# A hybrid decoder step on one core: GpSimd's share of the mixer goes to VectorE

## The chip, the core and the metric

The kernel runs on one core of one Trainium2 chip. The core has TensorE (PE in the rows; its weight loads are PEld), VectorE (DVE), ScalarE (ACT), GpSimd (POOL) and SyncE (SP), which here only issues transfers. The metric is device time in microseconds (us) of one execution. Line numbers such as L716 are those of the kernel before.

## The reference, cut to what matters

One layer of a decoder, in float32, for 256 prompt tokens and 8 x 8 sampled tokens, 320 in all: a half feed-forward, a mixer, and another half feed-forward.

```
h = x + 1/2 * SwiGLU_1(RMSNorm(x))
z = RMSNorm(h) @ w_in      -> q | k | v | conv pair a, b
A: 16 heads of 64, three dilated patterns (128,1), (512,4), (2048,16);
   sampled queries read cache_k, cache_v (8 x 2048 rows of 1024)
B: u = a * sigmoid(b); causal depthwise conv of 31 taps; LayerNorm; swish
h = h + concat(A, B) @ w_out
y = h + 1/2 * SwiGLU_2(RMSNorm(h))
```

## The kernel before, in words

**Products.** Features lie on the partitions, the 320 tokens beside each other. A weight piece is loaded by SyncE (`raw`, L276), rounded by ScalarE (`wh`, L238), and the rest is formed by VectorE (`wl = raw - wh`, L239); TensorE then does three matmuls per tile (L299 to L301). A piece is 128x1024 in the feed-forwards and 128x512 in the mixer. The mixer's pieces have four `raw` buffers and three pairs `wh`, `wl`, so a late `wl` holds back both TensorE and the next load. Counted over the whole program, pieces 281 to 312 make k, 313 to 376 the conv pair, 377 to 408 v, 409 to 440 the half of w_out that multiplies the conv branch, and 441 to 472 the other half.

**Beside the products.** After every piece of k, conv, v and of w_out's first half, `pump` puts some steps of the sampled tokens' attention and five entries of `bg`, the convolution's list, into the program. One step of attention is one tile of 128 cache rows, 512 KB. A *far* tile (L511 to L513, six per batch, ring `kf` of three buffers) holds keys that one query each sees: GpSimd multiplies it with the query `qr` (L512) and VectorE sums over the head (L513). A *near* tile goes through TensorE (L534 to L547), a value tile too (`vn`, L610, L614). Between batches come the softmax (L562 to L571) and two spread products `af` and `px` on GpSimd (L520, L571).

**The convolution.** For each of eight channel tiles, 21 taps are `cacc += w * u` on VectorE (L716; the first is L714); ten are products on ScalarE (L721), added up by GpSimd (L725, L749). The sampled tokens' taps are one product of 992 columns on GpSimd (L734) and a sum on VectorE (L736), twice per tile. Behind the last tile stand the steps of the LayerNorm: sums over the tiles (L810, even tiles on VectorE, odd ones on GpSimd), mean, centring (L826), root (L834, L836), scaling (L839) and swish (L840). Only then can w_out's first half begin: its operands are the split conv tiles `ch`, `cl` (L238, L239).

**The rest of GpSimd's work in the mixer.** The products with the norm's root and with the sine for q and k (L447, L455), a copy of the sampled columns (L458), the gate's product (L791), half of the scaling (L839), and clearing and filling a small tile `z` (L568, L569).

**Order.** The program is recorded in the order above; a scheduler then sets each engine's fixed order with a timeline of its own, attention steps first (their priority is raised), `bg` behind. Each engine works its list strictly in that order.

Of the kernel before, what the change touches and what calls it, by code (L numbers as in the profile page):

```python
# [22 lines left out]
TD = 8  # L23
# [19 lines left out]
PTAPS = 10  # L43
# [32 lines left out]
def shape_constants():  # L76
    """Tables that depend on the shapes alone, side by side in one array."""
    parts = []

    def put(name, a):  # L80
        off = sum(p.shape[1] for p in parts)
        _CW[name] = (off, a.shape[1])
        parts.append(np.ascontiguousarray(a, dtype=np.float32))

    p = np.arange(P)
    put("ident", np.eye(P))
    put("blk64", (p[:, None] // HD == p[None, :] // HD) / HD)
    inv = np.power(np.float32(10000.0), -np.arange(HD // 2, dtype=np.float32) / np.float32(HD // 2)).astype(np.float32)
    pos = np.concatenate([np.arange(SEQ), np.tile(PAST + np.arange(TD), NB)]).astype(np.float32)
    ang = (inv[p % (HD // 2)][:, None] * pos[None, :]).astype(np.float32).astype(np.float64)  # L90
    sgn = np.where(p % HD < HD // 2, -1.0, 1.0)[:, None]
    put("cos", np.cos(ang))
    put("sin", np.sin(ang) * sgn)
    q = np.arange(P)[:, None]
    put("pmask", np.concatenate([_bias(q - np.arange(P)[None]), _bias(P + q - np.arange(2 * P)[None])], 1))
    t = (p % TD)[:, None]
    idx = np.concatenate([FAR + np.arange(NNEAR * P), PAST + np.arange(TD)])
    far = 16 * np.arange(NFAR * 16)
    put("smask", np.concatenate([_bias(PAST + t - idx[None, :]), _bias(PAST - far[None, :] + 0 * t)], 1))
    put("tmask", t == np.arange(TD)[None, :])  # L100
    put("msel", (p // TD)[:, None] == np.arange(16)[None, :])
    f = np.arange(256)
    put("dmask", (p // TD % 4)[:, None] == (f // HD)[None, :])
    put("sel", ((p // 32 * TD + p % TD)[:, None] == np.arange(32)[None, :]))
    return np.concatenate(parts, 1)
# [5 lines left out]
def block(ctx, tc, A, O):  # L111
# [41 lines left out]
    class Norm:  # L153
        """Deferred RMSNorm: x*g goes on (split) at once, the reciprocal root is applied to the products."""
# [57 lines left out]
    def tables():  # L212
        """The other gains and the taps of the convolution, features on the partitions."""
# [34 lines left out]
    def defer(n, fn):  # L248
        """Trace fn n weight pieces further on, so that the tensor engine has work while its operands are made."""
        later.append([n, fn])  # L250
# [12 lines left out]
    class Feed:  # L263
        """Weight pieces of nkp row tiles x 256 columns in the order of their use: loads run la pieces ahead of the
        products, splits ls pieces."""
# [22 lines left out]
    def gemm(feed, nk, hi, lo, evac, after=None):  # L288
        """Two column tiles of the weights (nk row tiles) times the split activations."""
# [108 lines left out]
    # fixed buffers in turn: their users follow in the order of the program  # L398
# [12 lines left out]
    # the rows of the conv state that stay  # L411
    nc.sync.dma_start(O["new_conv_sample"][0][:, 0:ST - TD, :], A["state_conv"][0][:, TD:ST, :])

# [1 line left out]
    def out3(src, dsts):  # L415
        """Three token blocks of a [feature, token] tile, transposed, to dsts."""
# [11 lines left out]
    if True:  # L428
# [12 lines left out]
        def qk_norm(i, zq, sq, goff, is_q, d):  # L441
# [5 lines left out]
            nc.gpsimd.tensor_tensor(zq, zq, sd, op=ALU.mult)  # L447
# [7 lines left out]
            nc.gpsimd.tensor_tensor(rot, rot, sin, op=ALU.mult)  # L455
            r = rp.tile([P, T], F32, name="qk", bufs=5)
            nc.vector.tensor_tensor(r, t1, rot, op=ALU.add)
            nc.gpsimd.tensor_copy((qsT if is_q else ksT)[:, i, :], r[:, SEQ:T])  # L458
# [23 lines left out]
    sa = mix.enter_context(tc.tile_pool(name="sa", bufs=2, side="right"))  # L482
    ck = A["cache_k"][0].rearrange("b s h d -> b s (h d)")
# [20 lines left out]
    def far_scores(b, out):  # L504
        """Row p of a far tile holds keys that only query p % 8 sees: products on the vector engines."""
# [3 lines left out]
        for n in range(NFAR):  # L509
            kn = sa.tile([P, AW], F32, name="kf", bufs=3)  # L510
            nc.sync.dma_start(kn, rows(ck, b, n))  # L511
            nc.gpsimd.tensor_tensor(kn, kn, qr, op=ALU.mult)  # L512
# [5 lines left out]
    def far_sums(S, sf):  # L518
        af = sa.tile([P, NFAR * 16, TD], F32, name="af", bufs=1)
        nc.gpsimd.tensor_tensor(af, bc(sf), tmb, op=ALU.mult)  # L520
# [38 lines left out]
    def soft(S):  # L559
# [7 lines left out]
        z = sa.tile([P, 2 * TS - TD], F32, name="z")  # L567
        nc.gpsimd.memset(z, 0.0)  # L568
        nc.gpsimd.tensor_copy(z[:, TS - TD:TS], sm[:, SNEW:SFAR])  # L569
        px = sa.tile([P, NFAR * 16, TD], F32, name="px", bufs=1)  # L570
        nc.gpsimd.tensor_tensor(px, bc(sm[:, SFAR:SW]), tmb, op=ALU.mult)  # L571
# [52 lines left out]
    def late_values():  # L624
        """The new keys' part of the batches whose rows came before v was there."""
# [68 lines left out]
    cst = ExitStack()  # L694
    cp = cst.enter_context(tc.tile_pool(name="cp", bufs=2))
    cprod = deque(cp.tile([P, 384], F32, name=f"cprod{i}", bufs=1) for i in range(3))
    csum = deque(cp.tile([P, 384], F32, name=f"csum{i}", bufs=1) for i in range(2))
# [8 lines left out]
    def conv_taps(i, u):  # L706
        a = cacc[i]
        ap, bias = a[:, 0:SEQ], gains[:, DWB + i:DWB + i + 1]
        s2 = {}

        def tap(j):
            w, src = dww[:, i, j:j + 1], u[:, j:j + SEQ]
            if j == 0:
                nc.vector.tensor_scalar(ap, src, w, bias, op0=ALU.mult, op1=ALU.add)  # L714
# [3 lines left out]
        def ptap(j):  # L718
            first = "c" not in s2
            t = turn(csum if first else cprod)[:, 0:SEQ]  # L720
            nc.scalar.activation(t, u[:, j:j + SEQ], AF.Copy, bias=0.0, scale=dww[:, i, j:j + 1])  # L721
            if first:
                s2["c"] = t
            else:
                nc.gpsimd.tensor_tensor(s2["c"], s2["c"], t, op=ALU.add)  # L725

        def stap(h):
            """The decoded tokens of four batches: all taps of their windows at once."""
# [5 lines left out]
            nc.gpsimd.tensor_tensor(pr4, win, w, op=ALU.mult)  # L734
# [5 lines left out]
        nd = CW - PTAPS  # L740
        for j in range(nd):
            bg.append(lambda j=j: tap(j))
            k = (j + 1) * PTAPS // nd - j * PTAPS // nd
            for x in range(k):
                bg.append(lambda x=j * PTAPS // nd + x: ptap(nd + x))
            if j in (3, 9):
                bg.append(lambda j=j: stap(j > 3))
        def close():
            nc.gpsimd.tensor_tensor(ap, ap, s2["c"], op=ALU.add)  # L749
            norm_add("m", a, i)  # L750

        bg.append(close)
# [22 lines left out]
    def conv_in(g, after):  # L775
# [7 lines left out]
        def ev_b(j, ps):  # L783
# [7 lines left out]
            nc.gpsimd.tensor_tensor(uc, at[j], t, op=ALU.mult)  # L791
# [10 lines left out]
    def norm_add(key, x, i):  # L802
        """Sums over the channel tiles, the even ones on one engine, the odd ones on the other."""
        e = nc.gpsimd if i % 2 else nc.vector
        k = key + str(i % 2)
        if i < 2:
            norm[k] = tmp.tile([P, T], F32, name="n" + k, tag=("ssa", "sd")[i % 2], bufs=1)
            e.tensor_copy(norm[k], x)
        else:
            e.tensor_tensor(norm[k], norm[k], x, op=ALU.add)  # L810

    def norm_mean(key):
        m = mtile("mu")
        for i in range(2):
            nc.tensor.matmul(m[:, 0:T], onesC, norm[key + str(i)], start=i == 0, stop=i == 1)
        return m[:, 0:T]

    def conv_norm():
# [19 lines left out]
        def act(i):  # L838
            (nc.gpsimd if i % 2 else nc.vector).tensor_tensor(cacc[i], cacc[i], s["r"], op=ALU.mult)  # L839
# [179 lines left out]
```

## Time and profile before

| | |
|---|---|
| time, median of 3 runs | 2650.08 us (2642.7 to 2655.48) |
| profiled execution, its span | 2650.1 us |
| TensorE busy | 2536.2 us, 96% |
| VectorE busy | 1445.5 us, 55% |
| ScalarE busy | 1031.1 us, 39% |
| GpSimd busy | 447.6 us, 17% |
| granted TensorE clock, mean | 0.980 |

The profiled execution's span equals the median to 0.1 us, so a sum made against the span can be read as a sum against the median. Shares over the whole span say little: the feed-forwards lie before about 970 us and after about 1710 us, with TensorE busy throughout, and the mixer between them looks different. It is read stage by stage.

### The profile page before, as it was taken

The numbers are of one execution on the slowest core, as the hardware profiler recorded it, in microseconds if no ns is written. First come the engines' busy times: TensorE is split into PE (matmuls) and PEld (weight loads), VectorE is DVE, ScalarE is ACT, GpSimd is POOL, SyncE is SP. The second block draws the span as 40 slices with busy tenths as digits, with TensorE's granted clock in tenths as the row PEclk, the third lists the DMA queues.
The fourth block names the chain that finished last, engine by engine and source line by source line (L and its number), as shares of the span: only waits on it lengthen the run. The fifth ranks groups of instructions, "written<-read, shape, count | busy, mean of one in ns | idle before, by whom it ended". The sixth has DMA issues, their size and how long they took to land. (4 is left out here: it accounts for less than half of the span.)

```text
span 2650.1 us, 43147 instructions
## 1 busy us (share of the span) xinstructions
PE 2536.2 (96%) x17612; PEld 2424.5 (91%) x17612; DVE 1445.5 (55%) x1785; ACT 1031.1 (39%) x1597; POOL 447.6 (17%) x392
## 2 busy tenths in 40 slices
PE   7999999999999999888878899999999999999999
PEld 6999999999999998777666675999999999999999
DVE  5444444444444576979899744644444444444443
ACT  4333333333323456555434434533333333333333
POOL 3000000000000123746666400200000000000000
PEclk9999999999999999899989899999999999999999
DMA  6544444444444455978888966454444444544443
GB/s 191 162 151 151 147 149 151 151 151 149 149 149 151 151 156 166 237 217 232 232 216 232 259 186 185 146 153 150 151 152 148 151 149 149 151 151 150 148 150 119
DMA packets 385543, 443.21 MB, mean 167 GB/s; under 512 B 17274, under 2 KB 362290, under 8 KB 385328
## 3 DMA queue, kind: packets, MB, share of 16 engines
q1 hardware_dynamic: 385344, 440.45, 56.1%
q8 instruction: 138, 2.26, 0.4%
q14 instruction: 61, 0.50, 0.1%
HBM read 432.39 MB, written 8.71 MB: 166 GB/s over the span
## 5 line engine op out<-in xcount | busy, mean ns | idle before, releaser
L239 DVE TENSOR_TENSOR wl<-raw,wh 128x1024 fp32r<-128x1024 f32 (+1 forms) x736 | 868.6, 1182 | 933.9 <-ACT wh L238 921.7
L238 ACT CAST wh<-raw 128x1024 fp32r<-128x1024 f32 (+1 forms) x736 | 688.0, 936 | 1275.8 <-PE acc L300 1088.0
L299 PE MATMUL acc<-xh_a,wh 128*128 128x320 f32 x1408 | 437.2, 311 | 1.5 <-ACT wh L238 1.5
L300 PE MATMUL acc<-xl_a,wh 128*128 128x320 f32 x1408 | 437.4, 311 | 0.0
L301 PE MATMUL acc<-xh_a,wl 128*128 128x320 f32 x1408 | 436.9, 310 | 0.0
L301 PE MATMUL acc<-hh,wl 128*128 128x320 f32 x1408 | 435.5, 309 | 0.0
L299 PE MATMUL acc<-xh_c,wh 128*128 128x320 f32 x1408 | 435.3, 309 | 0.0
L300 PE MATMUL acc<-xl_c,wh 128*128 128x320 f32 x1408 | 435.1, 309 | 0.0
L301 PE MATMUL acc<-xh_c,wl 128*128 128x320 f32 x1408 | 435.1, 309 | 0.0
L300 PE MATMUL acc<-hl,wh 128*128 128x320 f32 x1408 | 435.0, 309 | 0.0
L299 PE MATMUL acc<-hh,wh 128*128 128x320 f32 x1408 | 435.0, 309 | 0.0
L348 POOL TENSOR_TENSOR hm<-ut,sg 128x320 f32<-128x320 f32 x88 | 77.4, 880 | 1659.5 <-DVE ut L346 1659.5
L299 PEld LDWEIGHTS acc<-xh_a,wh 128*128 128x128 f32 x1408 | 265.9, 189 | 1.7 <-ACT wh L238 1.6
L300 PEld LDWEIGHTS acc<-xl_a,wh 128*128 128x128 f32 x1408 | 266.0, 189 | 0.3 <-issue 0.2
L301 PEld LDWEIGHTS acc<-xh_a,wl 128*128 128x128 f32 x1408 | 265.8, 189 | 0.5 <-DVE wl L239 0.2
L300 PEld LDWEIGHTS acc<-xl_c,wh 128*128 128x128 f32 x1408 | 264.4, 188 | 0.1
L299 PEld LDWEIGHTS acc<-xh_c,wh 128*128 128x128 f32 x1408 | 264.4, 188 | 0.1
L301 PEld LDWEIGHTS acc<-xh_c,wl 128*128 128x128 f32 x1408 | 264.4, 188 | 0.0
L300 PEld LDWEIGHTS acc<-hl,wh 128*128 128x128 f32 x1408 | 264.3, 188 | 0.0
L301 PEld LDWEIGHTS acc<-hh,wl 128*128 128x128 f32 x1408 | 264.3, 188 | 0.0
L299 PEld LDWEIGHTS acc<-hh,wh 128*128 128x128 f32 x1408 | 264.2, 188 | 0.0
L301 PE MATMUL acc<-xh_b,wl 128*128 128x320 f32 x640 | 205.5, 335 | 42.3 <-DVE wl L239 42.3
(214 smaller groups left out, 3016.5 us busy)
## 6 DMA issues: line engine op xcount, KB each, us to landing
raw<-ffn_w_gate SPq DMA_DIRECT2D x176, 512.0 KB, 3.6
raw<-ffn_w_up SPq DMA_DIRECT2D x176, 512.0 KB, 3.5
raw<-ffn_w_down SPq DMA_DIRECT2D x176, 512.0 KB, 3.5
vn<-cache_v SPq DMA_DIRECT2D x80, 512.0 KB, 6.6
raw<-w_in SPq DMA_DIRECT2D x128, 256.0 KB, 4.6
kf<-cache_k SPq DMA_DIRECT2D x48, 512.0 KB, 8.7
kn<-cache_k SPq DMA_DIRECT2D x32, 512.0 KB, 6.8
raw<-w_out SPq DMA_DIRECT2D x64, 256.0 KB, 5.0
```

Source lines behind the costliest of these rows:

```text
L238: nc.scalar.copy(dsth, src)
L239: nc.vector.tensor_tensor(dstl, src, dsth.bitcast(F32), op=ALU.subtract)
L299: nc.tensor.matmul(a, h, hi[kk], start=st, stop=False)
L300: nc.tensor.matmul(a, h, lo[kk], start=False, stop=False)
L301: nc.tensor.matmul(a, l, hi[kk], start=False, stop=sp)
L348: nc.gpsimd.tensor_tensor(m, t, sg[j], op=ALU.mult)
```

## The change

GpSimd no longer computes anything in the mixer. Its products, sums and spread products become VectorE instructions at the same places of the program; its small copies (L458, L569) and the first tap (L714) go to ScalarE. The ten ScalarE taps per channel tile with their GpSimd sums go away: all taps but the first are `cacc += w * u` on VectorE, so there are 30 per tile where there were 20. The sums over the channel tiles are one chain. The list `bg` has 34 entries per channel tile before and after. The pace of `pump`, the tiles, rings and loads are unchanged, and all loads stay in SyncE's queue. In the feed-forwards GpSimd keeps its work (L176, L348).

```
-            nc.gpsimd.tensor_tensor(zq, zq, sd, op=ALU.mult)
+            nc.vector.tensor_tensor(zq, zq, sd, op=ALU.mult)
...
-            nc.gpsimd.tensor_tensor(rot, rot, sin, op=ALU.mult)
+            nc.vector.tensor_tensor(rot, rot, sin, op=ALU.mult)
...
-            nc.gpsimd.tensor_tensor(kn, kn, qr, op=ALU.mult)
+            nc.vector.tensor_tensor(kn, kn, qr, op=ALU.mult)
...
-        nc.gpsimd.tensor_tensor(af, bc(sf), tmb, op=ALU.mult)
+        nc.vector.tensor_tensor(af, bc(sf), tmb, op=ALU.mult)
...
-        z = sa.tile([P, 2 * TS - TD], F32, name="z")
-        nc.gpsimd.memset(z, 0.0)
-        nc.gpsimd.tensor_copy(z[:, TS - TD:TS], sm[:, SNEW:SFAR])
+        z = turn(zbuf)
+        nc.scalar.copy(z[:, TS - TD:TS], sm[:, SNEW:SFAR])
...
-        nc.gpsimd.tensor_tensor(px, bc(sm[:, SFAR:SW]), tmb, op=ALU.mult)
+        nc.vector.tensor_tensor(px, bc(sm[:, SFAR:SW]), tmb, op=ALU.mult)
...
             if j == 0:
-                nc.vector.tensor_scalar(ap, src, w, bias, op0=ALU.mult, op1=ALU.add)
+                nc.scalar.activation(ap, src, AF.Identity, bias=bias, scale=w)
             else:
                 nc.vector.scalar_tensor_tensor(ap, src, w, ap, op0=ALU.mult, op1=ALU.add)
...
-            nc.gpsimd.tensor_tensor(pr4, win, w, op=ALU.mult)
+            nc.vector.tensor_tensor(pr4, win, w, op=ALU.mult)
...
-        nd = CW - PTAPS
-        for j in range(nd):
+        for j in range(CW):
             bg.append(lambda j=j: tap(j))
...
-            if j in (3, 9):
-                bg.append(lambda j=j: stap(j > 3))
...
+            if j in (6, 14):
+                bg.append(lambda j=j: stap(j > 6))
+        bg.append(lambda: norm_add("m", a, i))
...
+            nc.vector.tensor_tensor(norm[key], norm[key], x, op=ALU.add)
...
-            (nc.gpsimd if i % 2 else nc.vector).tensor_tensor(cacc[i], cacc[i], s["r"], op=ALU.mult)
+            nc.vector.tensor_tensor(cacc[i], cacc[i], s["r"], op=ALU.mult)
```

The scheduler sets another order from it. First VectorE's list just behind the split of piece 402, in the third quarter of v. Before (`nv` are the LayerNorm's sums, `w` a result of v; the tiles' products are GpSimd's):

```order
L810 TENSOR_TENSOR nv_14015<-nv_14015,sq 128x320
L239 TENSOR_TENSOR wl<-raw,wh 128x512 x2
L848 TENSOR_TENSOR w_9196<-acc,rstd 128x320
L810 TENSOR_TENSOR nv_14015<-nv_14015,sq 128x320
L848 TENSOR_TENSOR w_9197<-acc,rstd 128x320
L513 TENSOR_REDUCE sf<-kf 128x16
```

VectorE at the same place now, where L714 is a tap, L514 the product of a far tile, L515 its sum and L826 a result of v:

```order
L238 TENSOR_TENSOR wl<-raw,wh 128x512
L515 TENSOR_REDUCE sf<-kf 128x16
L826 TENSOR_TENSOR w_9197<-acc,rstd 128x320
L714 SCALAR_TENSOR_TENSOR cacc_9177<-u_10900,dww,cacc_9177 128x256
L238 TENSOR_TENSOR wl<-raw,wh 128x512
L714 SCALAR_TENSOR_TENSOR cacc_9178<-u_10901,dww,cacc_9178 128x256
L714 SCALAR_TENSOR_TENSOR cacc_9179<-u_10899,dww,cacc_9179 128x256
L514 TENSOR_TENSOR kf<-kf,qr 128x1024
L515 TENSOR_REDUCE sf<-kf 128x16
L789 TENSOR_TENSOR nm<-nm,cacc_9177 128x320
```

At piece 402 the list before is already in the LayerNorm; the list now is in the taps of the fourth to sixth of eight channel tiles (cacc_9174 to cacc_9181).

The second place is VectorE's list where the last taps end and the LayerNorm begins. Before:

```order
L716 SCALAR_TENSOR_TENSOR cacc_9181<-u_10902,dww,cacc_9181 128x256
L810 TENSOR_TENSOR nm_11772<-nm_11772,cacc_9180 128x320
L239 TENSOR_TENSOR wl<-raw,wh 128x512
L716 SCALAR_TENSOR_TENSOR cacc_9181<-u_10902,dww,cacc_9181 128x256 x3
L239 TENSOR_TENSOR wl<-raw,wh 128x512 x2
L513 TENSOR_REDUCE sf<-kf 128x16
L826 TENSOR_TENSOR cacc_9174<-cacc_9174,mu 128x320
```

And now, where L804 is the centring and nm the sum over the channel tiles:

```order
L714 SCALAR_TENSOR_TENSOR cacc_9180<-u_10900,dww,cacc_9180 128x256
L714 SCALAR_TENSOR_TENSOR cacc_9181<-u_10901,dww,cacc_9181 128x256
L789 TENSOR_TENSOR nm<-nm,cacc_9180 128x320
L714 SCALAR_TENSOR_TENSOR cacc_9181<-u_10901,dww,cacc_9181 128x256 x5
L789 TENSOR_TENSOR nm<-nm,cacc_9181 128x320
L804 TENSOR_TENSOR cacc_9174<-cacc_9174,mu 128x320
L804 TENSOR_TENSOR cacc_9175<-cacc_9175,mu 128x320
```

Before, this stands between the splits of pieces 395 to 398, with ten more pieces of v to come. Now the split of piece 411, the third piece of w_out, stands ahead of it, and the next split of a piece comes only behind the whole LayerNorm.

## Rows read from the trace of the kernel before

**Rows 1.** Busy tenths of the page, 40 slices of the span each.
```profile
PE   7999999999999999888878899999999999999999
DVE  5444444444444576979899744644444444444443
POOL 3000000000000123746666400200000000000000
PEclk9999999999999999899989899999999999999999
```

**Rows 2.** Stretches of the mixer: length, busy us (instructions), granted clock, DMA share, GB/s.
```profile
core 0: us, PE busy (x) PEld busy (x) DVE busy (x) ACT busy (x) POOL busy (x), PEclk, DMA share, GB/s
1022.00:1124.00 102.00, 87.67 (x559) 78.85 (x557) 81.26 (x80) 53.93 (x114) 62.16 (x44) 0.91 0.89 241
1124.00:1357.00 233.00, 196.97 (x1589) 164.14 (x1590) 207.17 (x267) 120.34 (x266) 141.19 (x119) 0.94 0.80 219
1357.00:1453.00 96.00, 74.12 (x566) 59.81 (x560) 90.97 (x105) 38.98 (x91) 66.09 (x48) 0.91 0.91 240
1453.00:1507.00 54.00, 42.81 (x299) 35.72 (x298) 39.55 (x43) 27.14 (x57) 26.47 (x16) 0.84 0.99 249
1507.00:1661.00 154.00, 144.04 (x1119) 104.67 (x1118) 73.28 (x222) 59.88 (x160) 9.62 (x7) 0.97 0.73 202
```

**Rows 3.** What SyncE's queue waited for, 1124 to 1357: us, times, longest.
```profile
SPq L276 <- DVE wl L239: 62.9, 30, 10.2
SPq L276 <- DVE cacc L716: 34.3, 13, 5.4
```

**Rows 4.** VectorE by line and form, 976 to 1661.
```profile
L239 DVE TENSOR_TENSOR wl<-raw,wh 128x512 fp32r<-128x512 f32 x163 | 157.4, 971 | 51.5 <-ACT wh L238 42.4 <-ACT ah L238 4.9 <-issue 2.2
L716 DVE SCALAR_TENSOR_TENSOR cacc<-u,dww,cacc 128x256 f32<-128x256 f32 x160 | 134.3, 867 | 0.6
L513 DVE TENSOR_REDUCE sf<-kf 128x16 f32<-128x1024 f32 x48 | 57.8, 1204 | 17.1 <-POOL kf L512 17.1
L446 DVE RECIPROCAL w<-w 128x320 f32<-128x320 f32 x16 | 33.7, 2130 | 3.6 <-ACT w L445 3.6
```

**Rows 5.** VectorE's timeline, 1232 to 1244: start, us, what.
```profile
1236.60 2.06 DVE L716 SCALAR_TENSOR_TENSOR cacc<-u,dww,cacc 128x256 f32<-128x256 f32 x5
1238.69 0.69 DVE L239 TENSOR_TENSOR wl<-raw,wh 128x512 fp32r<-128x512 f32 x1
1239.31 1.85 DVE L716 SCALAR_TENSOR_TENSOR cacc<-u,dww,cacc 128x256 f32<-128x256 f32 x2
1241.08 1.23 DVE L239 TENSOR_TENSOR wl<-raw,wh 128x512 fp32r<-128x512 f32 x1
```

**Rows 6.** GpSimd's timeline, 1236 to 1244.
```profile
1235.73 0.79 POOL L725 TENSOR_TENSOR csum<-csum,cprod 128x256 f32<-128x256 f32 x1
1239.22 3.69 POOL L725 TENSOR_TENSOR csum<-csum,cprod 128x256 f32<-128x256 f32 x4 [2.69 <-ACT cprod L721]
```

**Rows 7.** GpSimd by line and form, 976 to 1661.
```profile
L512 POOL TENSOR_TENSOR kf<-kf,qr 128x1024 f32<-128x1024 f32 x48 | 121.5, 2535 | 66.9 <-DMA kf<-cache_k 29.9 <-DMA qr<-dqs 25.1 <-issue 4.2
L725 POOL TENSOR_TENSOR csum<-csum,cprod 128x256 f32<-128x256 f32 x72 | 62.3, 868 | 17.2 <-ACT cprod L721 14.2
```

**Rows 8.** VectorE by line and form, 100 to 900, in the first feed-forward.
```profile
L239 DVE TENSOR_TENSOR wl<-raw,wh 128x1024 fp32r<-128x1024 f32 x227 | 286.9, 1264 | 380.4 <-ACT wh L238 380.4
L239 DVE TENSOR_TENSOR hl<-hm,hh 128x320 fp32r<-128x320 f32 x38 | 16.7, 479 | 0.0
```

**Rows 9.** VectorE's timeline, 1452 to 1508.
```profile
1453.23 0.48 DVE L848 TENSOR_TENSOR w<-acc,rstd 128x320 f32<-128x320 f32 x1
1462.95 2.15 DVE L836 RECIPROCAL mu<-sd 128x320 f32<-128x320 f32 x1 [1.15 <-ACT sd L834]
1507.27 1.07 DVE L953 TENSOR_TENSOR y<-y,acc 128x320 f32<-128x320 f32 x2 [0.32 <-PE acc L301]
```

**Rows 10.** ScalarE's timeline, 1453 to 1508.
```profile
1461.10 1.28 ACT L834 ACT_TABLE_LOAD   x1
1462.39 0.53 ACT L834 ACTIVATE sd<-misc_mu,eps 128x320 f32<-128x320 f32 x1
1467.00 0.65 ACT L840 ACTIVATE cacc<-cacc,gains 128x320 f32<-128x320 f32 x1 [1.67 <-DVE cacc L839]
```

**Rows 11.** The chain that ended last, 1617 to 1661: start, us, what.
```profile
1633.40 6.40 DMA vn<-cache_v
1639.85 0.68 PE S L614 x8
```

More of the change, by code (lines that the diff above doesn't have):

```diff
@@ L42 @@
 SW = SFAR + NFAR * 16
-PTAPS = 10
 HPX = 300
@@ L454, in qk_norm @@
             nc.vector.scalar_tensor_tensor(t1, zq, gq, cos, op0=ALU.mult, op1=ALU.mult)
-            nc.gpsimd.tensor_tensor(rot, rot, sin, op=ALU.mult)
+            nc.vector.tensor_tensor(rot, rot, sin, op=ALU.mult)
             r = rp.tile([P, T], F32, name="qk", bufs=5)
             nc.vector.tensor_tensor(r, t1, rot, op=ALU.add)
-            nc.gpsimd.tensor_copy((qsT if is_q else ksT)[:, i, :], r[:, SEQ:T])
+            nc.scalar.copy((qsT if is_q else ksT)[:, i, :], r[:, SEQ:T])
             nc.sync.dma_start((dq if is_q else dk)[i], r[:, 0:SEQ])
@@ L482, in block @@
     sa = mix.enter_context(tc.tile_pool(name="sa", bufs=2, side="right"))
+    zbuf = deque(sa.tile([P, 2 * TS - TD], F32, name=f"z{i}", bufs=1) for i in range(2))
+    for z in zbuf:
+        nc.vector.memset(z, 0.0)
     ck = A["cache_k"][0].rearrange("b s h d -> b s (h d)")
@@ L695, in block @@
     cp = cst.enter_context(tc.tile_pool(name="cp", bufs=2))
-    cprod = deque(cp.tile([P, 384], F32, name=f"cprod{i}", bufs=1) for i in range(3))
-    csum = deque(cp.tile([P, 384], F32, name=f"csum{i}", bufs=1) for i in range(2))
     srow = deque(cp.tile([120, 2, P], F32, name=f"srow{i}", bufs=1) for i in range(2))
@@ L708, in conv_taps @@
         ap, bias = a[:, 0:SEQ], gains[:, DWB + i:DWB + i + 1]
-        s2 = {}
         def tap(j):
@@ L713, in tap @@
             if j == 0:
-                nc.vector.tensor_scalar(ap, src, w, bias, op0=ALU.mult, op1=ALU.add)
+                nc.scalar.activation(ap, src, AF.Identity, bias=bias, scale=w)
             else:
                 nc.vector.scalar_tensor_tensor(ap, src, w, ap, op0=ALU.mult, op1=ALU.add)
[L718 to L725, printed above, removed]
         def stap(h):
@@ L738, in stap @@
                 nc.scalar.activation(a[:, SEQ:T], a[:, SEQ:T], AF.Identity, bias=bias)
-        nd = CW - PTAPS
-        for j in range(nd):
+        for j in range(CW):
             bg.append(lambda j=j: tap(j))
-            k = (j + 1) * PTAPS // nd - j * PTAPS // nd
-            for x in range(k):
-                bg.append(lambda x=j * PTAPS // nd + x: ptap(nd + x))
-            if j in (3, 9):
-                bg.append(lambda j=j: stap(j > 3))
[L748 to L752, printed above, removed]
+            if j in (6, 14):
+                bg.append(lambda j=j: stap(j > 6))
+        bg.append(lambda: norm_add("m", a, i))
     def u_out(i, uc):
@@ L790, in ev_b @@
             uc = at[j]
-            nc.gpsimd.tensor_tensor(uc, at[j], t, op=ALU.mult)
+            nc.vector.tensor_tensor(uc, at[j], t, op=ALU.mult)
             nc.scalar.copy(u[:, ST:UW], uc[:, 0:SEQ])
@@ L802, in norm_add @@
     def norm_add(key, x, i):
[L804 to L808, printed above, removed]
+        if i == 0:
+            norm[key] = tmp.tile([P, T], F32, name="n" + key, tag="ssa", bufs=1)
+            nc.scalar.copy(norm[key], x)
         else:
-            e.tensor_tensor(norm[k], norm[k], x, op=ALU.add)
+            nc.vector.tensor_tensor(norm[key], norm[key], x, op=ALU.add)
     def norm_mean(key):
         m = mtile("mu")
-        for i in range(2):
-            nc.tensor.matmul(m[:, 0:T], onesC, norm[key + str(i)], start=i == 0, stop=i == 1)
+        nc.tensor.matmul(m[:, 0:T], onesC, norm[key], start=True, stop=True)
         return m[:, 0:T]
```

## The prediction

> **What bounds the kernel now.** I read the page's tenths first [rows 1]. TensorE is full in both feed-forwards, where only a fall of work on TensorE would help, and the change adds or takes none there. Between the 16th and the 25th slice TensorE drops to 7 and 8, VectorE rises to 7 to 9, GpSimd to 7, and the granted clock falls below 9 in places. So the mixer is looked at by stages [rows 2]. In the conv stage, 1124 to 1357, VectorE is busy 207 of 233 us, TensorE 197, and the transfers run at 219 GB/s where the stage from 1453 to 1507 reaches 249. SyncE's queue says why: in that stage it stood 62.9 us behind VectorE's splits and 34.3 us behind its taps, which free the buffers it loads into [rows 3]. VectorE bounds the conv stage and the first part of v (91 of 96 us); in k (241 GB/s) and in v (240) the transfers are near their limit too. From 1507 on TensorE is busy 144 of 154 us and VectorE 73.
>
> **VectorE's instructions are slow beside GpSimd's.** A tap takes 867 ns on the mean [rows 4]. With GpSimd idle, five in a row take 2.06 us, 0.41 us each from start to start; beside a running sum of GpSimd two take 1.85 us, and a split of 512 columns takes 1.23 us where it takes 0.69 us alone [rows 5, 6]. The Trainium skill (Perfetto Trace Analysis, Optimizing Scalar/DVE Operations) says both that a saturated VectorE may give work to GpSimd, and that the two share an SBUF read port, so that this might not help. The trace bears out the second sentence (1.85 us for two taps beside GpSimd). By the first alone the work that comes over would be pure addition, which is the fourth rival below.
>
> **What goes from VectorE.** 160 taps at 0.867 us become 0.47 us each (0.41 us to the next start and the usual 0.06 us by which they overlap), which is 63 us less. 163 splits at 0.971 us become 0.69 us, 46 us less. Some 45 sums and products of 320 columns run beside GpSimd too; I put them at 20 us. The eight first taps go to ScalarE, 8 us. Together about 137 us of busy time.
>
> **What comes to VectorE.** 48 far products of 1024 columns, which cost GpSimd 2.535 us each [rows 7]. VectorE has not done one; the nearest row is its split of the same width, 1.264 us [rows 8], and nothing in the row suggests it could be below the 1.204 us of the sum over the same tile [rows 4]: 48 x 1.26 = 60 us. 80 more taps, 38 us. 16 products of 992 columns at the same price per column, 1.2 us, 19 us. 16 spread products of 768 columns: the bounds are 0.69 us (512 columns) and 1.264 us (1024), I take the middle, 0.97 us, 16 us. 52 of 320 columns (16 and 16 for q and k, 8 gates, 4 scalings, 8 sums) at 0.479 us [rows 8], 25 us. Together about 158 us. So VectorE's busy time in the mixer changes by +21 us, and since back-to-back instructions overlap and there are about 190 more of them, its occupied time hardly at all. ScalarE loses 72 + 8 products and gains 24 small copies and 8 taps; it is at 120 of 233 us [rows 2], so this is worth nothing.
>
> What decides is where that work now stands. I price the new order with the undisturbed durations less the 0.06 to 0.08 us by which neighbours overlap, as the taps of [rows 5] do: tap 0.41, split 0.61, far product 1.2, sum of a far tile 1.13, 320 columns 0.40, reciprocal 2.07.
>
> **First term, up to the split of piece 402 (1022 to 1453 us before).** Loads stand in SyncE's list as before up to there, within a few tiles. VectorE's list has 153 taps, 41 far products, 56 sums of tiles, 16 of 992 columns, 121 splits, 12 reciprocals and some 120 smaller ones: 343 us, where 379 of the 431 us were busy. In k it is 82 us of 102, where 81 were busy, so nothing is gained. In the conv stage it is 162 us of 233: VectorE is no longer the bound. Next is the traffic: 233 us x 219 GB/s = 51 MB, at 249 GB/s 205 us; and TensorE, 197 us. So at best 28 us come back there. I take 20, because neither runs without gaps; in v, already at 240 GB/s, nothing. Against it stands that far products wait for their tiles: GpSimd stood 29.9 us for `kf` and 25.1 us for `qr` [rows 7], with nothing behind it but its own list. Now splits are queued behind a waiting product and TensorE behind the splits. Of these 55 us, 17.1 were already passed on to VectorE through the sums [rows 4], so the loss is between 0 and 38 us. I count none here, since the new list puts taps between load and product. Term: -20 us, bounds -50 and +20.
>
> **Second term, from piece 402 to the first sum of w_out's results (1453.23 to 1507.27, 54 us before [rows 9]).** Before, the taps are over here, and VectorE is busy 40 of 54 us. Now 87 of the 240 taps are left, with 7 far products, 8 sums of tiles, 12 splits, 36 sums, products and splits of 320 columns of the LayerNorm, the reciprocal and ten others: 36 + 8 + 9 + 7 + 15 + 2 + 4 = 81 us. The attention steps stand in front by their priority, the taps are pushed to the end. Nothing hides it: v's last splits are done, w_out's first half needs the conv tiles, and the next split of a weight stands behind the LayerNorm. The chain in it costs more than VectorE's work: mean and its copy, squares and their sums taking turns on two buffers, table load 1.28 us and root 0.53 us [rows 10], the 1.15 us until the reciprocal [rows 9], the first swish and its split. I put these gaps at 9 us, and 5 us at waits for the last far tiles. 95 us against 54: +41 us, bounds +27 (no gap at all) and +60.
>
> **Third term, from there on (1507 to 1661).** TensorE bounds it and does the same work; the far tiles are done, which takes a few us from VectorE where it has room: 0. In the tail behind w_out's first half TensorE's list has 40 value matmuls where it had 48, two tiles of 0.68 us each with their loads, of which the later ones waited 6.40 us [rows 11]: between 1 and 14 us, I take 5. From 1661 nothing changes.
>
> **Sum.** 2650.1 - 20 + 41 - 5 = 2666 us, 0.6% slower.
>
> **Rivals.** *Even:* the relief is worth more than 20 us, because the splits come earlier in k and v too. With -35 for the first term, 2650.1 - 35 + 41 - 5 = 2651. For it: VectorE is 88% busy to 1453. Against: 240 GB/s there. *Faster:* the transfers run ahead of 249 GB/s once buffers are freed on time, the whole stretch to 1453 gives 60 us, and VectorE arrives at the backlog early: 2650.1 - 60 + 35 - 5 = 2620. For it: 343 us of need in 431; against: 359 us of TensorE in the same stretch, part of it at the lower clock [rows 2]. It decides if piece 402 is split before about 1400 us. *VectorE's queue stands at loads:* the 38 us above fall on it in full, 2666 + 38 = 2704. For it: `qr` has one buffer; against: three `kf` buffers and taps in between. *No relief:* the splits and taps stay at 867 and 971 ns for another reason than GpSimd. Then VectorE has 158 us more with 60 us idle in the 485 us to 1507, so about 2650 + 100 = 2750. The taps alone and beside GpSimd speak against it [rows 5]. That GpSimd would go on computing in the mixer is excluded by the order: its list has none of these rows left.
>
> **How the numbers follow.** Forecast 0.50, even 0.26, faster 0.15, waiting queue 0.07, no relief 0.02. A difference under 0.5%, 13 us, can't be told from none by a measurement of this kernel: faster is below 2637, slower above 2663. The forecast's own range is 2655 to 2690, and a tenth of it (0.05) lies below 2663. So slower 0.45 + 0.07 + 0.02 = 0.54; same 0.05 + 0.23 = 0.28, with 0.03 of the even case below 2637; faster 0.15 + 0.03 = 0.18. The range 2630 to 2704 leaves out about half of the faster case and the far end of the two last ones.
>
> **What would show it.** Taps with a mean near 0.47 us and splits of 512 columns near 0.69 us in the mixer show the relief; means above 0.7 us prove that wrong. Far products near 1.26 us on VectorE show their price. The conv stage should fall from 233 to about 213 us at some 240 GB/s, with VectorE at three quarters. Between v and w_out VectorE should be busy some 30 us with taps alone while TensorE idles and the granted clock falls, with the first L953 of w_out about 95 us behind the split of piece 402. If that gap is below 65 us, or the first term beyond -50, the forecast is wrong.

## The result, and the profile after

The changed kernel takes 2695.41 us (2691.94 to 2701.63, four runs), the kernel before 2648.08 on the same chip: a ratio of 1.017, 95% interval 1.015 to 1.019. It is slower, by 47 us on the medians. The profiled execution after spans 2690.2 us, 40.1 more than the one shown before; it was the fastest of its four runs, and what follows accounts for the 40.1.

The page's tenths of the kernel after, which answer to [rows 1]:

```profile
PE   7999999999999999699884599999999999999999
DVE  5444444444444577868888744644444444444443
POOL 2000000000000110000000000100000000000000
PEclk9999999999999999799996699999999999999999
```

GpSimd's digits in the mixer are gone. TensorE has two holes it did not have: the 17th slice (6, clock 7), which is k, and the 22nd and 23rd (4 and 5, clock 6), between v and w_out. VectorE's groups in the mixer of the kernel after, 976 to 1701 (count | busy us, mean ns | idle before and its releasers):

```profile
L238 DVE TENSOR_TENSOR wl<-raw,wh 128x512 fp32r<-128x512 f32 x163 | 111.5, 686 | 71.5 <-ACT wh L237 63.4 <-issue 2.5 <-ACT pt L499 2.3
L714 DVE SCALAR_TENSOR_TENSOR cacc<-u,dww,cacc 128x256 f32<-128x256 f32 x240 | 105.0, 478 | 0.1
L514 DVE TENSOR_TENSOR kf<-kf,qr 128x1024 f32<-128x1024 f32 x48 | 58.4, 1221 | 28.8 <-DMA kf<-cache_k 18.8 <-DMA qr<-dqs 9.4 <-DVE w L445 0.2
L515 DVE TENSOR_REDUCE sf<-kf 128x16 f32<-128x1024 f32 x48 | 57.9, 1210 | 0.0
L723 DVE TENSOR_TENSOR kf<-u,dww 128x992 f32<-128x992 f32 x16 | 18.8, 1183 | 0.0
L522 DVE TENSOR_TENSOR af<-sf,tmask 128x768 f32<-128x768 f32 x8 | 7.6, 952 | 1.7 <-PE S L524 1.7
```

The prices came out as worked out: splits 686 ns (971 in [rows 4]), taps 478 (867), far products 1221 where 1.26 us was put. The far products stood 28.8 us for `kf` and `qr`, on the engine that also forms the splits; before, the far sums stood 17.1 us there for GpSimd [rows 4].

To see where time went, I count the splits of weight pieces on VectorE's timeline and take the starts of pieces 281 (first of k), 321 (eight pieces into the conv pair), 402 (third quarter of v) and 472 (last), and of the first sum of w_out's results. Stretches in us, of the profiled executions:

| stretch | before | after | forecast |
|---|---|---|---|
| k: 281 to 321 | 133.2 | 148.8 | no change |
| conv and v: 321 to 402 | 310.1 | 291.7 | -20 |
| 402 to the first w_out sum | 54.6 | 101.0 | +41 |
| from there to 472 | 193.1 | 191.5 | -5 |

+15.6 - 18.4 + 46.4 - 1.6 = +42.0; the start of piece 281 lies 2.2 us earlier, the rest is equal. The same stretches as windows (columns as in [rows 2]), first the kernel before: k, conv and v, the whole mixer:

```profile
1009.00:1142.00 133.00, 118.06 (x742) 107.81 (x740) 109.24 (x104) 71.40 (x148) 78.50 (x55) 0.91 0.78 210
1142.00:1453.00 311.00, 253.70 (x2051) 207.63 (x2052) 280.47 (x356) 149.89 (x335) 194.88 (x159) 0.93 0.84 228
1009.00:1661.00 652.00, 558.61 (x4207) 455.82 (x4206) 502.54 (x723) 308.31 (x698) 309.47 (x236) 0.93 0.81 220
```

and the kernel after: k, conv and v, the gap, and the whole mixer:

```profile
1007.00:1156.00 149.00, 118.93 (x732) 109.00 (x731) 119.41 (x152) 72.86 (x161) 0.00 (x0) 0.85 0.71 191
1156.00:1448.00 292.00, 246.48 (x2038) 205.51 (x2036) 230.07 (x384) 120.63 (x262) 0.24 (x3) 0.94 0.92 246
1448.00:1549.00 101.00, 49.49 (x301) 40.89 (x302) 84.85 (x167) 32.47 (x69) 0.00 (x0) 0.65 0.45 126
1007.00:1701.00 694.00, 559.00 (x4211) 459.71 (x4210) 505.00 (x923) 287.25 (x654) 0.24 (x3) 0.89 0.76 207
```

Read the two rows of the whole mixer first. GpSimd's 309.5 us are gone, and VectorE is busy 505.0 us where it was busy 502.5: the relief and the new work cancel, in 200 more instructions. TensorE's busy time is equal too. In the sum, the 42 us more are time in which VectorE and TensorE wait. By stages the work has moved: VectorE is busy 10 us longer in k (119.4 for 109.2), 50 us less in conv and v (230.1 for 280.5) and 45 us longer in the gap (84.9 for 39.6 [rows 2]).

In k, VectorE's groups that changed most; first before, 1009 to 1142:

```profile
L239 DVE TENSOR_TENSOR wl<-raw,wh 128x512 fp32r<-128x512 f32 x37 | 41.6, 1134 | 7.7 <-ACT wh L238 7.7
L513 DVE TENSOR_REDUCE sf<-kf 128x16 f32<-128x1024 f32 x18 | 21.6, 1198 | 5.3 <-POOL kf L512 5.3
L457 DVE TENSOR_TENSOR qk<-w,w 128x320 f32<-128x320 f32 x11 | 9.2, 836 | 2.2 <-POOL w L455 2.2
```

then after, 1007 to 1156:

```profile
L238 DVE TENSOR_TENSOR wl<-raw,wh 128x512 fp32r<-128x512 f32 x38 | 25.8, 682 | 11.5 <-ACT wh L237 10.0 <-DMA new_k_prompt<-stage 0.9 <-PE misc_kt L542 0.3
L514 DVE TENSOR_TENSOR kf<-kf,qr 128x1024 f32<-128x1024 f32 x18 | 21.8, 1220 | 11.0 <-DMA kf<-cache_k 6.1 <-DMA qr<-dqs 4.6 <-DVE w L445 0.2
L456 DVE TENSOR_TENSOR qk<-w,w 128x320 f32<-128x320 f32 x12 | 5.8, 483 | 0.0
L446 DVE TENSOR_TENSOR w<-w,w 128x320 f32<-128x320 f32 x12 | 5.6, 474 | 0.0
L454 DVE TENSOR_TENSOR w<-w,sin 128x320 f32<-128x320 f32 x11 | 5.3, 481 | 4.1 <-ACT w L451 4.1
```

The splits give back 15.8 us, but the far products bring 21.8 and the norm's products (L446, L454) 10.9. VectorE's idle time in k goes from 23.8 to 29.6 us, and most of that rise is the far products' waits for loads, 11.0 us where the far sums had waited 5.3.

In conv and v the transfers now run at 246 GB/s, and SyncE's queue stands far less behind VectorE (1156 to 1350, against 34.3 and 62.9 us in [rows 3]):

```profile
SPq L275 <- DVE cacc L714: 15.6, 15, 2.2
SPq L275 <- DVE wl L238: 11.7, 10, 3.3
```

The gap is the row with 0.65 of the clock and 126 GB/s. VectorE's timeline after, where its last taps end (start, us, what [idle before <- releaser]):

```profile
1491.04 8.40 DVE L714 SCALAR_TENSOR_TENSOR cacc<-u,dww,cacc 128x256 f32<-128x256 f32 x21
1499.35 0.48 DVE L789 TENSOR_TENSOR nm<-nm,cacc 128x320 f32<-128x320 f32 x1
1499.75 8.40 DVE L714 SCALAR_TENSOR_TENSOR cacc<-u,dww,cacc 128x256 f32<-128x256 f32 x21
...
1511.07 0.49 DVE L789 TENSOR_TENSOR nm<-nm,cacc 128x320 f32<-128x320 f32 x1
1513.60 3.30 DVE L804 TENSOR_TENSOR cacc<-cacc,mu 128x320 f32<-128x320 f32 x8 [2.05 <-ACT mu L801]
1516.83 4.06 DVE L789 TENSOR_TENSOR nv<-nv,sq 128x320 f32<-128x320 f32 x7
1523.72 2.15 DVE L814 RECIPROCAL mu<-sd 128x320 f32<-128x320 f32 x1 [2.83 <-ACT sd L812]
1525.91 3.30 DVE L817 TENSOR_TENSOR cacc<-cacc,mu 128x320 f32<-128x320 f32 x8
...
1544.86 0.69 DVE L238 TENSOR_TENSOR wl<-raw,wh 128x512 fp32r<-128x512 f32 x1 [3.23 <-ACT wh L237]
...
1548.65 0.49 DVE L931 TENSOR_TENSOR y<-y,acc 128x320 f32<-128x320 f32 x1
```

87 taps are behind piece 402, as counted. From the last tile's sum (1511.07) to w_out's first sum lie 37.6 us: the LayerNorm, with no product of a weight beside it until its end. Before, its sums and its centring stood between the splits of v (VectorE's order before, in the section on the change). TensorE's waits in the same window (us, times, longest):

```profile
PE acc L298 <- DVE w L826: 24.6, 2, 18.9
PE misc_mu L793 <- DVE nm L789: 23.4, 1, 23.4
```

The second is the LayerNorm behind the taps. The first is not: these are results of v that stand behind far products and taps in VectorE's list. TensorE's 18.9 us lie between these two:

```profile
1454.22 0.48 DVE L826 TENSOR_TENSOR w<-acc,rstd 128x320 f32<-128x320 f32 x1
1473.32 0.48 DVE L826 TENSOR_TENSOR w<-acc,rstd 128x320 f32<-128x320 f32 x1
```

### The profile page after: what moved, and what is told of

Same layout as the page of the kernel before. It is cut to its first block, busy times and chain, and to the rows that moved or that the text cites. A ratio compares the mean times of both kernels' runs of the same rounds, so it can differ in the third digit from the quotient of the medians.

```text
span 2690.2 us, 42892 instructions
## 1 busy us (share of the span) xinstructions
PE 2534.2 (94%) x17608; PEld 2426.0 (90%) x17608; DVE 1447.6 (54%) x1989; ACT 1008.0 (37%) x1551; POOL 128.8 (5%) x148
## 4 chain that ended last, share of the span: by engine, by line
PE 83%; DMA 9%; DVE 5%; ACT 1%; issue 1%; POOL 0%; SPq 0%; ACTq 0%; DVEq 0%
PE acc L300 26%; PE acc L298 26%; PE acc L299 26%; DMA vn<-cache_v 4%; DMA raw<-w_in 3%; DMA kf<-cache_k 2%; DVE cacc L714 1%; PE S L615 1%; DVE sf L515 1%; PE misc_kt L542 1%; DVE wl L238 1%; DVE kf L514 1%; PE S L549 1%; PE misc_pp L919 0%; ACT wh L237 0%
## 5 line engine op out<-in xcount | busy, mean ns | idle before, releaser
L238 DVE TENSOR_TENSOR wl<-raw,wh 128x1024 fp32r<-128x1024 f32 (+1 forms) x736 | 821.4, 1117 | 951.4 <-ACT wh L237 939.7
L298 PE MATMUL acc<-xh_b,wh 128*128 128x320 f32 x640 | 212.8, 334 | 46.1 <-DVE w L826 24.6
L300 PE MATMUL acc<-xh_b,wl 128*128 128x320 f32 x640 | 200.8, 335 | 18.4 <-DVE wl L238 18.4
```

What stands on the lines that cost most here:

```text
L238: nc.vector.tensor_tensor(dstl, src, dsth.bitcast(F32), op=ALU.subtract)
L298: nc.tensor.matmul(a, h, hi[kk], start=st, stop=False)
L300: nc.tensor.matmul(a, l, hi[kk], start=False, stop=sp)
```

## The experiments

All were timed against the kernel before on their own chip. Theory C: the taps are late because the scheduler's timeline is paced by the one dependent chain. Its rival A: only the amount of VectorE's work counts. Theories for k: D, far products wait for their tiles in VectorE's list; Q, the products of q's and k's norm stand in that list. P: VectorE and GpSimd slow each other. L: the LayerNorm alone behind the taps is what costs. The recorded expectations use some letters otherwise: e1 calls its rival F; in e2 and e3 the theory of the waiting far products is W, and D there is the rival that the transfers bound k; from e7 on D is the waiting far products; in e4 the rival of P is N. Each edit also gets an order of its own from the scheduler. The stretches of all runs, in us as above:

| run | k | conv, v | 402 to sum | sum to 472 | time | ratio (95%) |
|---|---|---|---|---|---|---|
| before | 133.2 | 310.1 | 54.6 | 193.1 | 2648.1 | 1 |
| the change | 148.8 | 291.7 | 101.0 | 191.5 | 2695.4 | 1.017 (1.015-1.019) |
| e1 two chains | 145.1 | 297.9 | 83.1 | 193.3 | 2679.1 | 1.0105 (1.0084-1.0126) |
| e2 four kf | 143.2 | 300.4 | 97.2 | 190.4 | 2691.1 | 1.0149 (1.0131-1.0167) |
| e3 far on GpSimd | 143.1 | 296.4 | 95.9 | 196.8 | 2686.4 | 1.0132 (1.0109-1.0154) |
| e4 GpSimd beside | 209.2 | 305.8 | 99.8 | 197.1 | 2783.0 | 1.0492 (1.0469-1.0515) |
| e5 five chains | 146.4 | 309.9 | 69.0 | 193.8 | 2678.9 | 1.0119 (1.0097-1.014) |
| e6 five, far, q/k | 139.7 | 322.1 | 51.7 | 194.8 | 2665.2 | 1.0067 (1.005-1.0085) |
| e7 q/k on GpSimd | 142.4 | 292.5 | 101.7 | 191.1 | 2690.6 | 1.0168 (1.0145-1.019) |
| e8 before, q/k moved | 141.3 | 311.6 | 58.4 | 191.3 | 2662.3 | 1.0055 (1.0035-1.0076) |
| e9 before, taps moved | 135.0 | 307.6 | 76.2 | 194.6 | 2674.3 | 1.0093 (1.0076-1.011) |
| e10 before, far moved | 143.5 | 312.7 | 65.0 | 188.9 | 2672.4 | 1.0088 (1.0071-1.0105) |
| e11 no LayerNorm | 147.7 | 312.5 | 94.3 | 155.3 | 2658.0 | 1.003 (1.0016-1.0044) |
| e12 before, taps in four chains | 132.0 | 339.1 | 42.2 | 180.7 | 2659.7 | 1.0044 (1.0026-1.0061) |

VectorE's list in k is the same in the change, e1, e5 and e11, which took 145.1 to 148.8, and the same in before, e9 and e12, which took 132.0 to 135.0; so much one profiled execution leaves open there. The stretches are of the profiled execution, the time is the median; in e11 the profiled one was the longest of ten (2668.9 us), in e12 the shortest of six (2653.5).

**e1, two chains.**

```
+                d = b2 if j % 2 else ap
+                    nc.vector.scalar_tensor_tensor(d, src, w, d, op0=ALU.mult, op1=ALU.add)
...
+            nc.vector.tensor_tensor(ap, ap, b2, op=ALU.add)
```

> The changed kernel, but each conv tile's taps run in two chains of 15 (even taps into cacc, odd ones into a second buffer, first of each on ScalarE), added at the end: VectorE has 8 taps fewer and 8 additions more. Theory C: the second term (101 us from the split of piece 402 to the first sum of w_out, 54 before) is a backlog that comes from the order, which paces each tile's taps by one chain of 30 dependent instructions; with two chains the taps stand earlier, the gap falls to about 65 us and the time from 2695 to about 2665 us. Rival F: VectorE simply has too much work up to there; then piece 402 comes later by what the gap loses, and the time stays within 8 us of 2695.

The gap fell by 18 us to 83.1, the time by 16. The direction is C's, the size half of it.

**e2, four kf buffers.**

```
-            kn = sa.tile([P, AW], F32, name="kf", bufs=3)
+            kn = sa.tile([P, AW], F32, name="kf", bufs=4)
```

> The changed kernel with four buffers for far tiles instead of three. Theory W: the first term gave 5 us instead of 20 because VectorE's queue stands 28.8 us at far products whose tile or query has not landed; a fourth buffer takes away over half of the 18.8 us at tiles, k to piece 321 falls from 149 to about 140 us, time about 2685. Rival D: the transfers bound this stretch and the waits are only their sign; time within 5 us of 2695, the waits move elsewhere.

The time is 4 us less, as the rival expected, and the far products' idle time in the mixer is 26.2 us where it was 28.8. In k itself none of it is for `kf` any more (6.8 us are for `qr`), and k is 143.2 us, near W's 140; but VectorE's list in k has another order here too, and in conv and v the waits for `kf` rise to 17.0 us from 12.7. A fourth buffer moved the waits more than it removed them.

**e3, far products on GpSimd.**

```
-            nc.vector.tensor_tensor(kn, kn, qr, op=ALU.mult)
+            nc.gpsimd.tensor_tensor(kn, kn, qr, op=ALU.mult)
```

> The changed kernel with the 48 far products back on GpSimd, all else moved. Theory W: VectorE loses 58 us of products and most of the 28.8 us of waits, and gets back slow taps and splits beside 115 us of GpSimd (about 45 us); k to piece 321 as before the change (about 135 us), time about 2665. Rival D: k stays at 149 us, and the time at 2690 or above, because what VectorE gains in products it loses on taps.

k is 5.7 us shorter than in the change (2.0 below the shortest run of the same k) and the time 9, but taps rise to 603 ns and splits to 790. That is between the two expectations.

**e4, GpSimd busy for nothing.** The change, plus 192 products of 512 columns on GpSimd that nobody reads; the clearing of the three `u` tiles goes to VectorE.

```
+            for _ in range(2 if nb else 0):
+                nc.gpsimd.tensor_tensor(gd[0], gd[0], gd[1], op=ALU.mult)
```

> The changed kernel with 192 products of 512 columns on GpSimd that nothing else reads or waits for (about 250 us, from the end of q on), beside the same VectorE work. Theory P (the two slow each other): taps and splits that run beside them take over 1 us on the mean, those after them 0.48 and 0.69 us, and the time rises by 30 to 80 us. Rival N (the slow instructions before came from waits or buffers of GpSimd's real work): taps 0.48 us throughout, time within 8 us of 2695.

VectorE's groups in e4 where those products run, 1020 to 1228 (L435 reads `acc` from PSUM, where TensorE's results lie; the others read tiles in SBUF, the core's working memory):

```profile
L238 DVE TENSOR_TENSOR wl<-raw,wh 128x512 fp32r<-128x512 f32 x37 | 53.6, 1459 | 3.5 <-ACT wh L237 3.5
L514 DVE TENSOR_TENSOR kf<-kf,qr 128x1024 f32<-128x1024 f32 x18 | 34.8, 1949 | 0.0
L445 DVE RECIPROCAL w<-w 128x320 f32<-128x320 f32 x12 | 25.2, 2123 | 0.8 <-ACT w L444 0.8
L515 DVE TENSOR_REDUCE sf<-kf 128x16 f32<-128x1024 f32 x18 | 21.5, 1202 | 0.0
L446 DVE TENSOR_TENSOR w<-w,w 128x320 f32<-128x320 f32 x12 | 16.9, 1413 | 0.0
L435 DVE TENSOR_TENSOR w<-acc,rstd 128x320 f32<-128x320 f32 x12 | 5.7, 476 | 0.0
```

P is shown: splits take 1459 ns instead of 686 and products of 320 columns 1413 instead of 469, while reciprocals and sums, which read one tile, keep their time. Taps can't tell: GpSimd's products end at 1282 us, when three taps had run. The time rises by 88 us, more than the 30 to 80 expected. So the relief is real; the other runs say why it is not a gain.

**e5, five chains**, as e1 with chain j mod 5.

> The change, with each channel tile's taps in five chains instead of one: tap j goes to chain j mod 5, the five first taps are ScalarE's, and four sums on VectorE close the tile. VectorE has 32 taps less and 32 sums of 256 columns more, so its amount of work is unchanged. Its list now has the last tap behind the split of piece 393 (411 with one chain), the centring of the LayerNorm from piece 405 (411). Theory C (the taps are late because the scheduler's timeline is paced by the one dependent chain, not because VectorE lacks time): no tap behind piece 402, first w_out sum about 65 us behind the split of piece 402 (101 with one chain, 83 with two), piece 402 itself up to 5 us later since the taps now stand in front of it, time about 2660. Rival A (amount: the work that came to VectorE has to be done before w_out in any order): what is gained behind piece 402 is lost ahead of it, piece 402 split near 1475 instead of 1448, time 2685 to 2695.

Both sides are half right. No tap is left behind piece 402 and the gap falls to 69.0, but piece 402 comes 16.6 us later. Conv and v of e5:

```profile
1154.00:1464.00 310.00, 255.30 (x2043) 212.82 (x2042) 264.10 (x477) 132.98 (x298) 0.24 (x3) 0.91 0.87 231
```

VectorE is busy 264 us where the change had 230, and the traffic falls from 246 to 231 GB/s: with the taps done in time this stretch takes as long as before (309.9 against 310.1 us), so the 18.4 us that the change gained here were lent by the taps it put off. e1 stands between the two (297.9, gap 83.1). The order still counts: with about the same work on VectorE, conv, v and gap together take 378.9 us here and 392.7 in the change, and the kernel is 16 us faster. What is left above the kernel before is 13.2 us in k and 14.4 in the gap.

**e6, five chains, far products and q's and k's products on GpSimd** (the edits of e3, e5 and e7).

> Five chains as in the run before, and the 48 far products and the products and small copies of q's and k's norm back on GpSimd. Theories C and Q together (taps in front, and in k neither waiting far products nor products of the norm in VectorE's list): k stage from split 281 to 321 about 135 us (148.8 in the change), first w_out sum about 55 us behind piece 402, conv and v 5 us longer than in the change because splits and taps stand beside GpSimd again (splits 790 ns, taps 600): 2695 - 14 - 46 + 5 = 2640, a little below the kernel before. Rival P (the mutual slowdown takes it back): conv and v 20 us longer than in the change, 2655 or more, not faster than before.

P's side: splits 860 ns, conv and v 30.4 us longer than in the change, 2665 us. The gap is 51.7. k is 139.7, still 6.5 above before.

**e7, q's and k's products on GpSimd.**

```
-            nc.vector.tensor_tensor(zq, zq, sd, op=ALU.mult)
+            nc.gpsimd.tensor_tensor(zq, zq, sd, op=ALU.mult)
...
-            nc.vector.tensor_tensor(rot, rot, sin, op=ALU.mult)
+            nc.gpsimd.tensor_tensor(rot, rot, sin, op=ALU.mult)
...
-            nc.scalar.copy((qsT if is_q else ksT)[:, i, :], r[:, SEQ:T])
+            nc.gpsimd.tensor_copy((qsT if is_q else ksT)[:, i, :], r[:, SEQ:T])
```

> The change, with only the products with the norm's root and with the sine and the small copies of q and k back on GpSimd. Theory Q (in k, what costs is that these stand in VectorE's and ScalarE's lists between the evacuations and the splits): k stage from split 281 to 321 about 136 us (148.8 in the change, 133.2 before), time about 2683. Rival D (it is the far products that wait for their tiles in VectorE's list): k stage stays at 145 to 149 us, time within 5 us of the change, 2695.

k falls by 6.4 us (2.7 below the shortest run of the same k), half of what Q expected; the time is within 5 us of the change, as D expected. Neither alone.

**e8, the kernel before with only those moved** (the reverse edit there).

> The kernel before, with only the products with the norm's root and with the sine of q and k moved to VectorE and the small copies to ScalarE. Theory Q: k stage from split 281 to 321 goes from 133.2 to about 145 us and the time to about 2660. Rival D: k stage stays at 132 to 136, time within 4 us of before, 2650.

k 141.3 and 2662.3 us: what moved with q's and k's norm costs k time by itself, 8.1 us where 12 were expected. The window of k:

```profile
1007.00:1148.00 141.00, 118.55 (x729) 108.68 (x728) 118.84 (x129) 73.54 (x161) 50.32 (x22) 0.87 0.73 201
```

It is work, not waiting: VectorE is busy 9.6 us longer than before and idle 1.6 us less.

**e9, the kernel before with only the taps moved.** 

```
-        for j in range(nd):
+        for j in range(CW):
             bg.append(lambda j=j: tap(j))
-            k = (j + 1) * PTAPS // nd - j * PTAPS // nd
-            for x in range(k):
-                bg.append(lambda x=j * PTAPS // nd + x: ptap(nd + x))
...
-            nc.gpsimd.tensor_tensor(ap, ap, s2["c"], op=ALU.add)
```

> The kernel before, with only the taps moved: all 31 taps of a channel tile on VectorE in one chain, the ten ScalarE products and GpSimd sums gone, everything else of the mixer on GpSimd as before. Its list on VectorE has 212 of 240 taps ahead of piece 402 (153 of 240 in the change, 160 of 160 before) and the whole LayerNorm behind the split of piece 411. Theory L (what costs is the LayerNorm standing alone behind the taps): k stage from split 281 to 321 stays at 133 us, 402 split some 5 us earlier or at the same time, first w_out sum 80 to 90 us behind it (54.6 before), time about 2675. Rival A (only the amount of VectorE's work counts, and 80 taps at 0.41 against the relief of 160 taps and the splits come out even): time within 6 us of before, 2650.

k 135.0, piece 402 1.1 us earlier, time 2674.3: L's numbers, with a gap of 76.2 us where 80 to 90 were expected. And taps still take 744 ns here, splits 936, because GpSimd keeps computing, the far products above all: a part of the change gets a part of the relief. C falls as the whole reason: with one chain, 212 taps stand ahead of piece 402 here and 153 in the change, so what else is in VectorE's list decides too.

**e10, the kernel before with only the far products moved** (the reverse of e3 there).

> The kernel before, with only the 48 far products moved to VectorE. Its list has 156 of 160 taps ahead of piece 402, but the centring of the LayerNorm only from piece 409 on (398 before). Theory D (in k the far products wait for their tiles in VectorE's list, ahead of splits): k stage 138 to 141 us instead of 133.2. Theory L: first w_out sum 75 us behind piece 402 instead of 54.6. Together about 2670. Rival A (amount: 48 x 1.2 us of products against what GpSimd's 121 us no longer slow): k 133, time within 6 us of before, 2650.

The time is the one expected by D and L, 2672, but in part by luck: k is above the 138 to 141 us expected and the gap, 65.0, is 10 us below the 75. The window of k, and VectorE's waits in it:

```profile
1009.00:1153.00 144.00, 119.46 (x739) 109.21 (x738) 114.03 (x124) 72.82 (x153) 38.23 (x41) 0.91 0.74 198
DVE kf L512 <- DMA qr<-dqs: 6.4, 1, 6.4
DVE kf L512 <- DMA kf<-cache_k: 3.9, 3, 2.5
```

VectorE stands 10.3 us for loads where it had stood 5.3 us for GpSimd's far products. k is 10.3 us longer, which is between 4 and 5 us more of busy time (114.0 for 109.2 in these windows) and some 6 more of idle time; that both figures are 10.3 is chance.

**e11, no LayerNorm.** Sums, mean, centring, root and scaling are left out of the change.

```
-        return ([mean] + [lambda i=i: cen(i) for i in range(8)] + [var] + [lambda i=i: act(i) for i in range(8)])
+        return [nop] * 10 + [lambda i=i: act(i) for i in range(8)]
```

> The change, with the LayerNorm left out (no sums over the channel tiles, mean, centring, squares, root and scaling; the swish takes the taps' result). VectorE has 30 sums, centrings and scalings of 320 columns and one reciprocal less, 16 us; 78 taps are still behind piece 402. Theory L (of the 101 us behind piece 402 some 37 are the chain of the LayerNorm, in which VectorE mostly waits): first w_out sum about 65 us behind piece 402, time about 2660. Rival A (only VectorE's 16 us go): 85 us behind piece 402, time about 2679.

The time is L's, 2658 (2660 expected, 2679 by A), but not by the way I expected: the first w_out sum still comes 94.3 us behind piece 402. What changed is TensorE beside the taps (1467 to 1562 in e11):

```profile
1467.00:1562.00 95.00, 77.58 (x572) 60.12 (x564) 74.19 (x154) 33.82 (x68) 0.00 (x0) 0.73 0.76 207
```

It is busy 77.6 of 95 us, where the change had 49.5 of 101: without the LayerNorm each finished channel tile can be multiplied while the next tile's taps run, and the rest to piece 472 takes 155 us instead of 191. Against it, conv and v take 20.8 us longer than in the change. TensorE waited 22.7 us there for `wh` of ScalarE (7.9 in the change); the reason was not looked for, and that the time meets L's 2660 is in part luck. The LayerNorm is a barrier: it needs all tiles, so all late taps stand in front of w_out.

**e12, the kernel before with only the taps moved, in four chains**, the version to which e5 and e9 point.

> The kernel before, with only the taps moved as in the run with the taps alone, but each channel tile's taps in four chains (the four first ones on ScalarE, three closing sums on VectorE). Everything else of the mixer stays on GpSimd. VectorE's list has all taps ahead of piece 392 and the last scaling of the LayerNorm behind piece 403, as before. Theory L (with the taps alone the 24 us were the LayerNorm standing behind the backlog): first w_out sum about 55 us behind piece 402 (76.2 with one chain), k stage 133 to 135 us, time 2640 to 2652, not slower than before. Rival A (VectorE's amount: the taps, now in front, delay splits and far sums as they did with five chains, 16 us in conv and v): piece 402 split near 1466, time about 2664.

2659.7 us, 0.44% slower than before: nearer A's 2664 than L's 2640 to 2652. The LayerNorm is hidden (gap 42.2), k is as before, and conv and v take 339.1. All taps stand ahead of piece 392 in its list, and VectorE is busy 294 us in that stretch, where it was 280 of 311 before:

```profile
1140.00:1479.00 339.00, 269.47 (x2098) 221.72 (x2099) 293.93 (x433) 136.37 (x296) 132.95 (x83) 0.88 0.84 224
```

No version run here beats the kernel before.

## Why the prediction was wrong

**Right: direction, prices, the relief, the second term.** The relief of taps and splits, the far products' price, the 87 late taps, the fall of the clock and the LayerNorm behind piece 411 are as forecast. Conv and v gave 18.4 us, 20 were put; the conv stage (pieces 315 to 379) fell from 233 to 220 us, where 213 were expected, and v gave most of the rest. The second term is +46.4 for +41: VectorE was busy 84.9 us in the gap for 81, and idle 16.2 for 14. One premise of it was not so: "v's last splits are done". Five splits of v still stood behind far products and taps, 1479 to 1485. The third term is -1.6 for -5; it was not traced. VectorE's list to piece 402 as a whole was right too: 36 us less busy time were put, some 40 measured.

**Wrong: the first term's k.** The forecast was +16 us and the profiled execution shows +40.1; of the 24 us between them k has 15.6, the gap 5.4, the last stretch 3.4, conv and v 1.6; the 2.2 us ahead of piece 281 go the other way. The step that failed is "In k it is 82 us of 102, where 81 were busy, so nothing is gained", with "the loss is between 0 and 38 us. I count none here". Both halves failed. The count by stage was short: between the splits of pieces 284 and 315, those that the 102 us held, VectorE is busy 91 us after the change, and over the whole stretch 119.4 us where 109.2 were. And the waits were not nothing: VectorE is idle 5.8 us longer, as much as the waits at far tiles grew (11.0 us for 5.3). No engine is busy throughout k (VectorE 119 of 149 us, TensorE 119, transfers at 191 GB/s), and both parts stand in the stage's length, from 133.2 to 148.8 us.

Two causes were shown one at a time on the kernel before: the far products in VectorE's list cost k 10.3 us (e10), nearly half of it work and the rest waiting, and the norm's products 8.1 (e8), all of it work. They don't add: together they would be 18.4. Taken back out of the change, each gives 5.7 or 6.4 us (e3, e7), both 9.1 (e6); runs with one and the same k differ by up to 3.7 us, so these three are rough. The 6.5 us left in e6 were not told apart.

My reason for counting no waits was that taps stand between load and product. In k there are no taps yet; they begin with the conv tiles. The queue rival had the waiting, with 38 us as its bound; it is closer to the measured time than the forecast, but the far products' idle time was 28.8 us in all, and what it cost outside k is not separated.

**What I had not seen.** The -20 and the +41 are not two effects. Both come from the taps' place in VectorE's list: late taps let splits and loads run ahead in conv and v and leave the LayerNorm alone afterwards; earlier taps (e1, e5) shorten the gap and give the gain back, a third of it in e1 and all in e5. The amount of VectorE's work stays at some 503 us; a better order of it (e1, e5) saved 16 us of the 47, and none tried saved more. The *Even* and *Faster* rivals counted on VectorE's shorter list to piece 402; it came (40 us), but conv and v gave 18.4 us of it and k took 15.6 back. The Trainium skill (Perfetto Trace Analysis, Optimizing Scalar/DVE Operations) warns that work given to GpSimd may not help because the two share a read port. The mixer agrees in the sum: 309.5 us of GpSimd's work, with 21 us of ScalarE's, were worth 2.5 us of VectorE's.

The medians differ by 47 us and the profiled executions by 40; the 7 us lie within the spread of the runs (2691.94 to 2701.63) and were not traced.

## What to carry to other kernels

Where two engines slow each other, moving work from the one to the other can leave the busy time of the receiver unchanged, as here; ask then what the second queue was worth by itself, since a wait that stood in a queue of its own now stands ahead of everything else. A sum that is right for the whole can be wrong for a stage: count each stage's own list, from a named instruction to a named instruction. Then list the instructions in it that can wait for a load and what stands behind each. And before a barrier that needs all tiles, such as a norm over channels, count what the new order leaves unfinished there, because that part has nothing beside it.

## What the runs showed of the hardware

The mutual slowdown depends on VectorE's instruction. In e4, beside GpSimd products of two SBUF tiles, VectorE's instructions on two SBUF tiles take up to three times as long (320 columns: 1413 ns for 469; 512 columns: 1459 for 686; 1024 columns: 1949 for 1221). Those that read one SBUF tile are untouched: sum of 1024 columns 1202 ns for 1210, reciprocal 2123, and a product of 320 columns with one operand in PSUM 476. GpSimd's own products of 1024 columns took 2535 ns beside VectorE's work [rows 7], VectorE's 1221 with GpSimd idle.
